# Keeping VectorE's operands in PSUM between the dense stages of a state-space and convolution trunk

## The chip, the core and the metric

The kernel runs on one core of a Trainium2 chip. The metric is the device time of one launch in microseconds (us). TensorE (PE) multiplies matrices and writes its results to PSUM, of which the kernel uses eight banks of 128 partitions by 512 float32 numbers; all else lies in SBUF. VectorE (DVE), ScalarE (ACT) and GpSimd (POOL) work element by element; POOL's operands all lie in SBUF here. SyncE (SP) issues most transfers. Each engine takes its own instructions in order, and engines wait for each other by semaphores.

## The reference

Two layers on a sequence of 512 tokens with 1024 features, batch 1, all in float32:

```python
for i in range(DEPTH):                       # DEPTH = 2
    mods = c_act @ w_ada[i] + b_ada[i]
    sh1, sc1, g1, sh2, sc2, g2 = [m[:, None, :] for m in jnp.split(mods, 6, axis=-1)]
    h = modulate(rms_norm(x, norm1_g[i]), sh1, sc1)
    mix = s5_mixer(h, ...) if i % 2 == 0 else short_conv_mixer(h, ...)
    x = x + g1 * mix
    h = modulate(rms_norm(x, norm2_g[i]), sh2, sc2)
    x = x + g2 * swiglu(h, w_ffn_in[i], w_ffn_out[i])
return rms_norm(x, final_g)
```

`rms_norm` divides each token by the root of the mean of its squares. The state-space mixer ends in a gated product (GLU): `val, gate = jnp.split(y @ w_out, 2, axis=-1)` and `val * jax.nn.sigmoid(gate)`. The feed-forward part has 2816 hidden features.

## The kernel before, in words

The residual `xT` lies in SBUF with features on the partitions: eight blocks k of 128 features by 512 tokens. Every dense product is made of three matmuls on float32r halves (`acc3`, L336): the weights are split into a high part `wh` (copied by ACT, L119) and a low part `wl` (subtracted by DVE, or by POOL where `ws.eng` is `e.G`, L109), the activations likewise into `wide` or `hid` and `hlo`. `group` (L342) runs such products into tiles of PSUM called `o0` to `o3`; each tile is a bank. `SL` cuts the tokens: s = 0 is all 512, s = 1 and s = 2 are the halves of 256.

The first part, the state-space mixer with its scan, follows a list written out by hand (`ORDER`). Everything behind it is put in order by the framework's list scheduler, which goes by dependencies and by its own estimates, and which adds the waits. It treats two accesses to one PSUM bank as dependent whichever columns they touch. Behind the list come, in this order, the GLU projection, feed-forward 0, the convolution mixer, feed-forward 1 and the output.

Between two dense stages stands a normalization. So that TensorE does not stand idle there, `transition` (L456) halves the tokens: the last products of a stage are made for s = 1 and then for s = 2 (`tail`), and while those for s = 2 run, the norm of s = 1 is worked out (`Norm`, L426). `fix` adds a finished tile to `xT` (`resid`, L423, or `glu`, L556) and adds its squares to `acc` (`square`, L415). When all eight blocks are in, `sums` (L432) makes the sum over features by a matmul with ones into a bank called `ssq`, `rsqrt_small` (L262) takes the root in eleven small steps of DVE in the tile `nst`, `spread` puts the result on all partitions by a matmul into the bank `rstd`, and `apply` makes `nt` (DVE), `wide` (ACT) and `hlo` (DVE) for each k, from which the next stage's first products start, again s = 1 first (`first`), then s = 2. While s = 1 of the next stage runs, `hook2` works out the norm of s = 2. During transitions POOL subtracts the low weights.

The transition from the GLU projection into feed-forward 0 differs from the others. Its tail has only half the products per block, so its eight half tiles lie two to a bank (`halves`, L453): `o0` to `o3` for s = 1, `t20` to `t23` for s = 2. Blocks 2, 3, 6 and 7 are finished there. For each of them `glu` adds the partial sums `part` to value `pv` and gate `pg`, takes the sigmoid of the gate (ACT, L563), multiplies (DVE), adds to `xT` (DVE, L565) and squares. A chain of these steps for one block and one token half is called a unit below. The units use `pv` and `pg` of tiles `o0`/`o1`, `o0`/`o1` again (second half of the banks), `o2`/`o3` twice, then `t20`/`t21` twice and `t22`/`t23` twice. Blocks 4, 5, 0 and 1 are finished before, at full width, and there POOL adds three of the squares (`GE`).

Of the kernel before, what the change touches and what calls it, by code (L numbers as in the profile page):

```python
# [12 lines left out]
ALU = mybir.AluOpType  # L13
# [4 lines left out]
D = 1024  # L18
# [240 lines left out]
    return y, ops  # L259


def rsqrt_small(e, n, src, scale):  # L262

    h, y, t = e.nst[:, 0, 0:n], e.nst[:, 1, 0:n], e.nst[:, 2, 0:n]
    e.ts(h, src, scale / 2, EPS / 2, ALU.mult, ALU.add)
    e.ts(y.bitcast(I32), h.bitcast(I32), -0.5, float(0x5F3759DF - 0x80400000), ALU.mult, ALU.add)
    for _ in range(3):
        for c in range(n):
            q = slice(c, c + 1)
            e.stt(t[:, q], y[:, q], y[:, q], h[:, q], ALU.mult, ALU.mult)  # L270
        e.stt(y, t, 1.5, y, ALU.subtract, ALU.mult)
    return y
# [3 lines left out]
def hybrid_trunk(ctx: ExitStack, tc, x, c, norm1_g, norm2_g, w_ada, b_ada,  # L276
# [3 lines left out]
    e = common(tc, ctx)  # L280
# [11 lines left out]
    mods, xT = e.mods, e.xT  # L292
# [38 lines left out]
    SL = (slice(0, T), slice(0, TH), slice(TH, T))  # L331

    def width(s):
        return T if s == 0 else TH
# [7 lines left out]
    def group(units, nk, rhs, s, tiles=None, kouter=False, hook=None, first=True, last=True):  # L342

        if tiles is None:
            tiles = [e.ps(f"o{j}") for j in range(2 * len(units))]
        outs = [t[:, 0:width(s)] for t in tiles]
        ks = [(u, kk) for u in range(len(units[0])) for kk in range(units[0][u][0].shape[1])]
        run = lambda j, i: acc3(outs[j], units[j // 2][ks[i][0]], ks[i][1], (j % 2) * P, rhs(i, s),
                                first and i == 0, last and i == len(ks) - 1)
        if kouter:  # L350
            for i in range(len(ks)):
                for j in range(len(tiles)):
                    run(j, i)
                if hook:
                    hook(i)
        else:
            for j in range(len(tiles)):
                for i in range(len(ks)):
                    run(j, i)
                if hook:  # L360
                    hook(j)
        return tiles

    def getu(npairs, nk, interleaved):

        t = ws.get(npairs * nk)
        if interleaved:
            return [[t[k * npairs + q] for k in range(nk)] for q in range(npairs)]
        return [[t[q * nk + k] for k in range(nk)] for q in range(npairs)]

    if 1:
# [5 lines left out]
        def half(kh, tiles=None, first=True, last=True):  # L377

            return group(getu(2, 1, True), 1, lambda k, s: yrhs(4 * kh + k, s), 0, tiles=tiles, kouter=True,
                         first=first, last=last)  # L380
# [25 lines left out]
        tiles = part[2]  # L406
# [3 lines left out]
        def ft(tag, n=T, dt=F32):  # L410
            return fp.tile([P, n], dt, tag=tag, name=tag)

        accs = fp.tile([P, T], F32, tag="acc", bufs=1, name="acc")

        def square(k, s, init=False, eng=None):  # L415
            if init:
                A.activation(out=accs[:, SL[s]], in_=xT[:, k, SL[s]], func=AF.Square)
            else:
                q = ft("sq")[:, 0:width(s)]
                A.activation(out=q, in_=xT[:, k, SL[s]], func=AF.Square)  # L420
                e.add(accs[:, SL[s]], accs[:, SL[s]], q, eng)

        def resid(ps, g, k, s):  # L423
            e.stt(xT[:, k, SL[s]], ps[:, 0:width(s)], g[:, k:k + 1], xT[:, k, SL[s]], ALU.mult, ALU.add)

        class Norm:  # L426
# [5 lines left out]
            def sums(self):  # L432
                self.ps = e.ps("ssq")
                o = (self.s - 1) * TH
                for b in range(2):
                    e.mm(self.ps[:, b:b + 1], accs[:, o + b * P:o + b * P + P], e.ones1[:, 0:1], True, True)
                self.y = rsqrt_small(e, 2, self.ps[:, 0:2], 1.0 / D)

            def spread(self):
                self.r = e.ps("rstd")  # L440
# [12 lines left out]
        def halves(name):  # L453
            return [t[:, h * TH:h * TH + TH] for t in (e.ps(f"{name}{j}") for j in range(4)) for h in range(2)]

        def transition(tail, fix, gs, sh, first, n=4):  # L456


# [6 lines left out]
            for j in range(n):  # L465
                fix(j, tiles, 1)
            t2 = [e.ps(f"t2{j}") for j in range(4)] if n == 4 else halves("t2")

            def hook(j):
                if j == (0 if n == 4 else 3):  # L470
                    n1.sums()
                    ada.finish()
                if j == (2 if n == 4 else 6):
                    n1.spread()
                    n1.apply([0, 1])
                fix(j, t2, 2)
                if j == n - 1:
                    n1.apply(range(2, 8))
# [16 lines left out]
        class Ffn:  # L495
# [30 lines left out]
            def fix(self, j, tiles, s, k=None):  # L526
                k = 4 + j if k is None else k
                resid(tiles[j], mods[(self.i, 5)], k, s)
                square(k, s, k == 0)

            def tail(self, s, hook, tiles=None):
                if s == 1:
# [23 lines left out]
        def glu(k, pv, pg, s, add=None):  # L556
            g = ft("sg")[:, 0:width(s)]
            pv, pg = pv[:, 0:width(s)], pg[:, 0:width(s)]
            if add:
                e.add(g, pg, add[1])  # L560
                e.add(add[0], pv, add[0])
                pg, pv = g, add[0]
            A.activation(out=g, in_=pg, func=AF.Sigmoid)  # L563
            e.mul(g, g, pv)
            e.stt(xT[:, k, SL[s]], g, mods[(0, 2)][:, k:k + 1], xT[:, k, SL[s]], ALU.mult, ALU.add)  # L565
            square(k, s, k == 4, GE if s == 0 else None)

        GE = e.G
        ws.eng = e.G
        ada.finish()  # L570
        half(1, tiles=tiles, first=False)
        for q in range(2):
            glu(4 + q, tiles[q], tiles[2 + q], 0)
        tiles = half(1)
        for q in range(2):
            glu(q, tiles[q], tiles[2 + q], 0, (part[0][:, q], part[0][:, 2 + q]))
# [8 lines left out]
        def glu_fix(j, tiles, s):  # L585
            q, o = j % 4 - 2, (1, 3)[j // 4]
            if q >= 0:
                glu(2 * o + q, tiles[j - 2], tiles[j], s, (part[o][:, q, SL[s]], part[o][:, 2 + q, SL[s]]))
# [52 lines left out]
        for o in range(PAIRS):  # L641
            if o:
                if o == 2:
                    zbig(1)
                tiles = group(getu(2, 2, True), 2, rhs, 0, kouter=True)
# [7 lines left out]
        def conv_fix(j, tiles, s, k=None):  # L653
            k = 4 + j if k is None else k
            resid(tiles[j], mods[(1, 2)], k, s)
            square(k, s, k == 0)

        for o in range(2):
            tiles = group(getu(1, 2, False), 2, zrhs, 0, kouter=True)
            for j in range(2):  # L660
                conv_fix(j, tiles, 0, 2 * o + j)
            ada.step(16)
# [8 lines left out]

        f1 = Ffn(1)
        hi, lo, rhs = transition(conv_tail, conv_fix, mods[(1, 4)], mods[(1, 3)], f1.first)
        f1.body(rhs, 0)

# [30 lines left out]
        tiles = f1.tail(1, None)  # L706
# [761 lines left out]
```

## Time and profile before

| what | value |
|---|---|
| time, median of 3 runs | 1162.95 us (1160.84 to 1164.36) |
| time of the profiled execution | 1161.99 us |
| its span, first to last instruction | 1160.2 us |
| TensorE busy in the span | 1105.0 us, 95% |
| VectorE busy | 644.9 us, 56% |
| ScalarE busy | 384.6 us, 33% |
| GpSimd busy | 180.6 us, 16% |
| mean granted TensorE clock | 0.986 |

The span is what the profiler sees between the first and the last instruction, and the device time lies 1.8 us around it. The clock is the share of full speed that was granted to TensorE. An idle time in brackets behind a row says how long the engine stood before that instruction and whose end released it. An engine's busy time says little here by itself: what counts is where TensorE stands still or runs at half clock.

### The profile page before, as it was taken

To read this page: it belongs to the slowest core of one execution; us is meant where nothing else is said; L and a number is where in the kernel's file an instruction comes from. 1 tells how busy PE (TensorE), PEld (TensorE's weight loads), DVE (VectorE), ACT (ScalarE), POOL (GpSimd) and SP (SyncE) were. 2 spreads that over 40 slices of the span, in tenths; PEclk is the share of its full clock that TensorE was granted. 3 is DMA by queue.
4 is the path that set the end of the run, shared out by engine and by line. 5 is a ranking of instruction groups with operands and counts; after the bars stand their busy time and mean duration, and the time that the engine had idled before them with its cause. 6 is when DMAs were issued, how large, how long until landed. Compare 5 with 4: busy or idle time off the path is not lost.

```text
span 1160.2 us, 16331 instructions
## 1 busy us (share of the span) xinstructions
PE 1105.0 (95%) x6516; PEld 932.1 (80%) x6516; DVE 644.9 (56%) x1250; ACT 384.6 (33%) x596; POOL 180.6 (16%) x134
## 2 busy tenths in 40 slices
PE   4788999899999999999999999999999999999996
PEld 2566778898888888888889888899888888888886
DVE  8898323975666267733687665757324324233244
ACT  4754344342231132222334242334223213222233
POOL 4797817400000000000050000031000000000000
PEclk9889999999999999999999999999999999999999
DMA  9337654218894398726723939512332332233102
GB/s 279 126 115 255 195 192 127 91 55 182 195 193 120 118 193 197 182 90 137 173 92 105 202 112 210 151 61 86 109 110 88 95 108 88 94 109 100 55 28 73
DMA packets 141851, 153.50 MB, mean 132 GB/s; under 512 B 8288, under 2 KB 129228, under 8 KB 141776
## 3 DMA queue, kind: packets, MB, share of 16 engines
q1 hardware_dynamic: 140672, 150.79, 48.3%
q10 hardware_dynamic: 816, 1.58, 0.5%
q8 instruction: 51, 0.84, 0.3%
q14 instruction: 24, 0.20, 0.1%
q0 software_dynamic: 288, 0.10, 0.1%
HBM read 147.99 MB, written 2.10 MB: 129 GB/s over the span
## 4 chain that ended last, share of the span: by engine, by line
PE 85%; DVE 11%; ACT 3%; issue 1%; DMA 0%; DVEq 0%; ACTq 0%
PE o L117 79%; PE t L117 2%; DVE sx L109 1%; DVE scq L109 1%; DVE sg L109 1%; DVE xT L115 1%; DVE hlo L115 1%; DVE acc L109 1%; PE gmm L117 1%; PE yps L117 1%; DVE sr L120 0%; PE xtp L118 0%; DVE scr L109 0%; DVE v L109 0%; ACT u L1202 0%
## 5 line engine op out<-in xcount | busy, mean ns | idle before, releaser
L117 PE MATMUL o<-wide,wh 128*128 128x512 f32 (+1 forms) x992 | 364.7, 371 | 1.8 <-ACT wide L450 1.8
L117 PE MATMUL o<-wide,wl 128*128 128x512 f32 (+1 forms) x992 | 363.8, 370 | 0.0
L117 PE MATMUL o<-hlo,wh 128*128 128x512 f32 (+1 forms) x992 | 354.9, 370 | 2.3 <-DVE hlo L115 2.2
L119 ACT ACTIVATE wh<-wr 128x1024 fp32r<-128x1024 f32 (+1 forms) x184 | 188.5, 1039 | 387.1 <-PE o L117 310.0
L109 DVE TENSOR_TENSOR wl<-wr,wh 128x1024 fp32r<-128x1024 f32 (+1 forms) x156 | 185.4, 1199 | 157.3 <-ACT wh L119 155.3
L117 PEld LDWEIGHTS o<-wide,wh 128*128 128x128 f32 x992 | 187.9, 189 | 33.2 <-ACT wide L450 2.6
L117 PEld LDWEIGHTS o<-wide,wl 128*128 128x128 f32 x992 | 187.9, 189 | 30.8
L117 PEld LDWEIGHTS o<-hlo,wh 128*128 128x128 f32 x992 | 182.9, 189 | 34.7 <-DVE hlo L115 3.1
L117 PE MATMUL o<-hid,wh 128*128 128x512 f32 (+1 forms) x704 | 205.6, 375 | 0.0
L109 POOL TENSOR_TENSOR wl<-wr,wh 128x1024 fp32r<-128x1024 f32 x28 | 68.5, 2465 | 571.6 <-ACT wh L119 561.8
L117 PEld LDWEIGHTS o<-hid,wh 128*128 128x128 f32 x704 | 129.3, 188 | 23.7
L117 PE MATMUL o<-hid,wl 128*128 128x512 f32 (+1 forms) x352 | 131.9, 375 | 0.0
L109 DVE TENSOR_TENSOR sg<-sg,o 128x512 f32<-128x512 f32 (+1 forms) x50 | 31.8, 644 | 167.0 <-PE o L117 164.2
L115 DVE SCALAR_TENSOR_TENSOR aacc<-ada,cper,aacc 128x256 f32<-128x256 f32 x217 | 108.4, 499 | 21.7 <-DMA ada<-in_w_ada_dram 15.8
L506 ACT ACTIVATE sg<-o 128x512 f32<-128x512 f32 (+1 forms) x48 | 26.8, 562 | 170.3 <-PE o L117 168.6
L117 PEld LDWEIGHTS o<-hid,wl 128*128 128x128 f32 x352 | 66.3, 188 | 11.9
L117 PE MATMUL o<-yT,wh 128*128 128x512 f32 (+1 forms) x256 | 73.0, 367 | 0.0
L115 DVE SCALAR_TENSOR_TENSOR xT<-o,mod,xT 128x512 f32<-128x512 f32 (+1 forms) x56 | 38.7, 693 | 56.6 <-PE o L117 56.4
L117 PEld LDWEIGHTS o<-yT,wh 128*128 128x128 f32 x256 | 46.1, 189 | 8.4 <-issue 0.4
L117 PE MATMUL o<-yT,wl 128*128 128x512 f32 (+1 forms) x128 | 46.5, 363 | 0.0
L420 ACT ACTIVATE sq<-xT 128x256 f32<-128x256 f32 (+1 forms) x44 | 20.6, 472 | 57.3 <-DVE xT L115 51.7
L109 DVE TENSOR_TENSOR acc<-acc,sq 128x256 f32<-128x256 f32 (+1 forms) x41 | 26.5, 647 | 13.3 <-ACT sq L420 13.1
(219 smaller groups left out, 1024.9 us busy)
## 6 DMA issues: line engine op xcount, KB each, us to landing
wr<-in_w_ffn_in_dram SPq DMA_DIRECT2D x88, 512.0 KB, 3.5
ada<-in_w_ada_dram SPq DMA_DIRECT2D x112, 256.0 KB, 9.2
wr<-in_w_ffn_out_dram SPq DMA_DIRECT2D x40, 512.0 KB, 3.7
gt<-in_w_ada_dram SPq DMA_DIRECT2D x12, 1024.0 KB, 5.4
wr<-in_conv_w_in_dram SPq DMA_DIRECT2D x24, 512.0 KB, 3.5
aw<-in_w_ada_dram SPq DMA_DIRECT2D x16, 512.0 KB, 8.8
wr<-in_ssm_w_out_dram SPq DMA_DIRECT2D x16, 512.0 KB, 6.4
wr<-in_conv_w_out_dram SPq DMA_DIRECT2D x8, 512.0 KB, 6.3
```

What stands on the lines that cost most here:

```text
L109: (eng or e.V).tensor_tensor(out=out, in0=a, in1=b, op=op)
L115: e.stt = lambda o, a, s, b, op0, op1: e.V.scalar_tensor_tensor(out=o, in0=a, scalar=s, in1=b, op0=op0, op1=op1)
L117: e.mm = lambda o, l, r, start, stop: e.PE.matmul(out=o, lhsT=l, rhs=r, start=start, stop=stop)
L119: e.cp = lambda o, i: e.A.activation(out=o, in_=i, func=AF.Copy)
L420: A.activation(out=q, in_=xT[:, k, SL[s]], func=AF.Square)
L506: A.activation(out=w, in_=g[:, 0:width(s)], func=AF.Silu)
```

## The change

Intermediate results of the transitions stay in the PSUM banks of tiles that are finished anyway, so that each of DVE's sums, products and residual steps has one operand in PSUM and one in SBUF, where some had both in SBUF. `rsqrt_small` keeps its scaled sum and its products in the bank `ssq` and only the root in `nst`. `square` lets ACT write the squares over the finished tile, and DVE adds them from there; POOL's three additions are DVE's now. `glu` adds the partial sums in place, in the banks of `pv` and `pg`, multiplies into `pv` and squares into `pg`.

```diff
-def rsqrt_small(e, n, src, scale):
-
-    h, y, t = e.nst[:, 0, 0:n], e.nst[:, 1, 0:n], e.nst[:, 2, 0:n]
+def rsqrt_small(e, n, ps, scale):
+
+
+    src, h, y, t = ps[:, 0:n], ps[:, 8:8 + n], e.nst[:, 1, 0:n], ps[:, 16:16 + n]
     e.ts(h, src, scale / 2, EPS / 2, ALU.mult, ALU.add)
...
-        def square(k, s, init=False, eng=None):
+        def square(k, s, ps, init=False):
+
             if init:
                 A.activation(out=accs[:, SL[s]], in_=xT[:, k, SL[s]], func=AF.Square)
             else:
-                q = ft("sq")[:, 0:width(s)]
+                q = ps[:, 0:width(s)]
                 A.activation(out=q, in_=xT[:, k, SL[s]], func=AF.Square)
-                e.add(accs[:, SL[s]], accs[:, SL[s]], q, eng)
+                e.add(accs[:, SL[s]], accs[:, SL[s]], q)
...
-                square(k, s, k == 0)
+                square(k, s, tiles[j], k == 0)
...
             if add:
-                e.add(g, pg, add[1])
-                e.add(add[0], pv, add[0])
-                pg, pv = g, add[0]
+                e.add(pg, pg, add[1])
+                e.add(pv, pv, add[0])
             A.activation(out=g, in_=pg, func=AF.Sigmoid)
-            e.mul(g, g, pv)
-            e.stt(xT[:, k, SL[s]], g, mods[(0, 2)][:, k:k + 1], xT[:, k, SL[s]], ALU.mult, ALU.add)
-            square(k, s, k == 4, GE if s == 0 else None)
-
-        GE = e.G
+            e.mul(pv, pv, g)
+            e.stt(xT[:, k, SL[s]], pv, mods[(0, 2)][:, k:k + 1], xT[:, k, SL[s]], ALU.mult, ALU.add)
+            square(k, s, pg, k == 4)
+
```

The scheduler puts the instructions in another order for it, on TensorE too. First VectorE in the units on `o2` and `o3`, in the tail for s = 1 of the GLU transition; `part` are the partial sums, `sg` the sigmoid or the product, `sq` the squares. Before:

```order
L109 TENSOR_TENSOR part3_2044<-o2_2290,part3_2044 128x256
L109 TENSOR_TENSOR acc_2083<-acc_2083,sq_2403 128x256
L109 TENSOR_TENSOR sg_2406<-o3_2291,part3_2044 128x256
L109 TENSOR_TENSOR sg_2415<-o3_2291,part3_2044 128x256
L109 TENSOR_TENSOR sg_2406<-sg_2406,part3_2044 128x256
L109 TENSOR_TENSOR sg_2415<-sg_2415,part3_2044 128x256
L115 SCALAR_TENSOR_TENSOR xT_70<-sg_2406,mod02_78,xT_70 128x256
L115 SCALAR_TENSOR_TENSOR xT_70<-sg_2415,mod02_78,xT_70 128x256
```

And in the changed kernel:

```order
L109 TENSOR_TENSOR o3_2288<-o3_2288,part3_2044 128x256
L109 TENSOR_TENSOR acc_2083<-acc_2083,o1_2286 128x256
L109 TENSOR_TENSOR o2_2287<-o2_2287,sg_2401 128x256
L115 SCALAR_TENSOR_TENSOR xT_70<-o2_2287,mod02_78,xT_70 128x256
L109 TENSOR_TENSOR o2_2287<-o2_2287,part3_2044 128x256
L109 TENSOR_TENSOR acc_2083<-acc_2083,o3_2288 128x256
L109 TENSOR_TENSOR t20_2417<-t20_2417,part1_1721 128x256
L109 TENSOR_TENSOR o3_2288<-o3_2288,part3_2044 128x256
L109 TENSOR_TENSOR t21_2418<-t21_2418,part1_1721 128x256
L109 TENSOR_TENSOR o2_2287<-o2_2287,sg_2409 128x256
L115 SCALAR_TENSOR_TENSOR xT_70<-o2_2287,mod02_78,xT_70 128x256
```

Before, the two units on a pair of banks go side by side, step by step. Now the second unit's addition to `o3` stands behind the first unit's last access to `o3`, the sum of squares.

Second, TensorE where the first norm comes back (`rstd`) in the same transition; `o0` to `o3` are then the first tiles of feed-forward 0. Before:

```order
L117 MATMUL t23_2427<-yT11_1982,wh15_2192 128x256
L117 MATMUL rstd_2544<-ident_67,nst_77 128x128 x2
L117 MATMUL t23_2427<-yT10_1981,wh15_2192 128x256
L117 MATMUL t23_2427<-yT10_1981,wl15_2193 128x256
L117 MATMUL t23_2427<-yT11_1982,wh15_2192 128x256
```

And in the changed kernel:

```order
L117 MATMUL t23_2420<-yT11_1982,wh15_2191 128x256
L117 MATMUL rstd_2535<-ident_67,nst_77 128x128 x2
L117 MATMUL o0_2622<-wide_69,wh16_2197 128x256
L117 MATMUL o0_2622<-wide_69,wl16_2198 128x256
L117 MATMUL o1_2623<-wide_69,wh16_2197 128x256
L117 MATMUL o1_2623<-wide_69,wl16_2198 128x256
L117 MATMUL o2_2624<-wide_69,wh17_2273 128x256
L117 MATMUL o2_2624<-wide_69,wl17_2274 128x256
L117 MATMUL o0_2622<-hlo0_2271,wh16_2197 128x256
```

The twelve products for the second half of `t23` have moved 44 rows back, into the first group of the feed-forward.

Third, TensorE and VectorE around the norm of s = 2. Before, TensorE makes its sums here, and the matmuls into `rstd` come 41 rows later, ahead of the products for s = 2:

```order
L117 MATMUL o3_2636<-wide_69,wl19_2610 128x256
L117 MATMUL ssq_2673<-ones1_68,acc_2083 128x1 x2
L117 MATMUL o0_2633<-hlo1_2275,wh18_2282 128x256
L117 MATMUL o1_2634<-hlo1_2275,wh18_2282 128x256
L117 MATMUL o2_2635<-hlo1_2275,wh19_2609 128x256
```

In the changed kernel both stand together behind the last product for s = 1:

```order
L117 MATMUL o3_2625<-wide_69,wl19_2599 128x256
L117 MATMUL o3_2625<-hlo1_2272,wh19_2598 128x256
L117 MATMUL ssq_2662<-ones1_68,acc_2083 128x1 x2
L117 MATMUL rstd_2712<-ident_67,nst_77 128x128 x2
L117 MATMUL o0_2782<-wide_69,wh16_2197 128x256
```

And VectorE there in the changed kernel; before, the steps of the root all stood ahead of the products `sg` of feed-forward 0:

```order
L109 TENSOR_TENSOR acc_2083<-acc_2083,t23_2420 128x256
L109 TENSOR_TENSOR sg_2772<-sg_2772,o2_2624 128x256
L109 TENSOR_TENSOR sg_2777<-sg_2777,o3_2625 128x256
L116 TENSOR_SCALAR ssq_2662<-ssq_2662 128x2
L116 TENSOR_SCALAR nst_77<-ssq_2662 128x2
L109 TENSOR_TENSOR hid0_2771<-sg_2772,hid0_2771 128x256
L115 SCALAR_TENSOR_TENSOR ssq_2662<-nst_77,ssq_2662 128x1
L109 TENSOR_TENSOR hid0_2771<-sg_2777,hid0_2771 128x256
L115 SCALAR_TENSOR_TENSOR ssq_2662<-nst_77,ssq_2662 128x1
L115 SCALAR_TENSOR_TENSOR nst_77<-ssq_2662,nst_77 128x2
```

So nothing of the feed-forward's first group is left behind the sums for TensorE to do, and VectorE takes four steps of that group's evacuation in between.

More of the change, by code (lines that the diff above doesn't have):

```diff
@@ L436, in sums @@
                     e.mm(self.ps[:, b:b + 1], accs[:, o + b * P:o + b * P + P], e.ones1[:, 0:1], True, True)
-                self.y = rsqrt_small(e, 2, self.ps[:, 0:2], 1.0 / D)
+                self.y = rsqrt_small(e, 2, self.ps, 1.0 / D)
             def spread(self):
@@ L655, in conv_fix @@
             resid(tiles[j], mods[(1, 2)], k, s)
-            square(k, s, k == 0)
+            square(k, s, tiles[j], k == 0)
         for o in range(2):
```

## The prediction

> **What bounds the kernel now.** The page says that TensorE is busy for 95% of the span and carries 85% of the chain that ended last.
>
> ```profile
> PE 1105.0 (95%) x6516; PEld 932.1 (80%) x6516; DVE 644.9 (56%) x1250; ACT 384.6 (33%) x596; POOL 180.6 (16%) x134
> PE 85%; DVE 11%; ACT 3%; issue 1%; DMA 0%; DVEq 0%; ACTq 0%
> ```
>
> So a shorter step of DVE is worth nothing by itself; what counts is when the results arrive for which TensorE stands. Next I cut the span at the places where TensorE stands. The first two columns are a stretch and its length, the third TensorE's busy time; the granted clock is the third number from the end.
>
> ```profile
> 62.71:66.12 3.41, 1.57 (x24) 1.12 (x18) 3.34 (x15) 0.59 (x1) 3.33 (x3) 1.00 0.17 44
> 66.12:69.54 3.42, 3.42 (x42) 3.15 (x42) 2.74 (x9) 1.68 (x3) 3.26 (x4) 0.50 0.80 240
> 223.14:226.55 3.41, 0.39 (x4) 0.20 (x2) 3.38 (x2) 0.51 (x1) 3.41 (x2) 1.00 0.26 83
> 226.55:233.38 6.83, 5.87 (x27) 5.87 (x28) 6.26 (x13) 4.04 (x9) 2.06 (x2) 0.50 0.35 112
> 250.00:585.00 335.00, 335.00 (x1542) 280.03 (x1541) 193.20 (x298) 90.62 (x114) 4.95 (x2) 1.00 0.67 159
> 585.00:620.00 35.00, 31.92 (x250) 30.36 (x249) 28.18 (x72) 14.12 (x28) 9.75 (x4) 1.00 0.25 79
> 602.02:605.43 3.41, 2.40 (x18) 1.99 (x18) 3.41 (x7) 1.77 (x4) 0.93 (x1) 1.00 0.66 213
> 605.43:608.84 3.41, 2.46 (x21) 2.26 (x20) 3.03 (x4) 0.85 (x3) 2.38 (x1) 1.00 0.13 43
> 800.00:1110.00 310.00, 310.00 (x1405) 258.31 (x1404) 107.61 (x121) 81.42 (x101) 0.00 (x0) 1.00 0.30 95
> ```
>
> In the dense stages TensorE has no gap, so what it loses in a transition comes off nowhere later. The transition at 585 to 620 loses 3.1 us. The GLU transition, 216 to 246, loses most, and its waits stand in TensorE's own timeline (start, length, in brackets the idle time before and its releaser):
>
> ```profile
> 211.40 0.28 PE L117 MATMUL o<-yT,wh 128*128 128x256 f32 x1
> 215.72 0.28 PE L117 MATMUL t<-yT,wh 128*128 128x256 f32 x1
> 216.65 0.58 PE L117 MATMUL ssq<-ones,acc 128*128 128x1 f32 x4 [0.66 <-DVE acc L109]
> 222.92 0.61 PE L117 MATMUL rstd<-ident,nst 128*128 128x128 f32 x4
> 227.51 0.58 PE L117 MATMUL t<-yT,wh 128*128 128x256 f32 x1 [3.98 <-DVE sg L109]
> 243.32 0.28 PE L117 MATMUL o<-wide,wl 128*128 128x256 f32 x1
> 243.44 0.28 PE L117 MATMUL o<-hlo,wh 128*128 128x256 f32 x1
> 245.31 0.39 PE L117 MATMUL o<-wide,wh 128*128 128x256 f32 x1 [1.15 <-ACT wide L450]
> ```
>
> That is 0.66 + 3.98 + 1.15 = 5.8 us of idling. The 3.98 also cost clock: the 3.41 us in which TensorE worked 0.39 were followed by 6.83 at half clock, with 5.87 us of work in them, of which half, 2.9 us, is lost. In all the stage loses 8.7. The other rows of that table price the clock: 1.57 us of work in a stretch of 3.41 led to half clock too, 2.40 did not. The shortest half-clock stretch costs 3.42/2 = 1.7.
>
> **The change part by part.** *POOL and DVE.* DVE and POOL in the same place:
>
> ```profile
> 215.42 0.42 DVE L109 TENSOR_TENSOR acc<-acc,sq 128x256 f32<-128x256 f32 x1
> 217.34 2.04 DVE L109 TENSOR_TENSOR sg<-sg,part 128x256 f32<-128x256 f32 x1
> 222.16 0.74 DVE L109 TENSOR_TENSOR part<-t,part 128x256 f32<-128x256 f32 x2
> 222.82 1.81 DVE L109 TENSOR_TENSOR sg<-sg,part 128x256 f32<-128x256 f32 x1
> 224.68 2.44 DVE L115 SCALAR_TENSOR_TENSOR xT<-sg,mod,xT 128x256 f32<-128x256 f32 x1
> 227.04 0.41 DVE L109 TENSOR_TENSOR sg<-t,part 128x256 f32<-128x256 f32 x1
> 231.87 2.40 DVE L109 TENSOR_TENSOR acc<-acc,sq 128x256 f32<-128x256 f32 x1 [0.19 <-ACT sq L420]
> 216.71 2.39 POOL L109 TENSOR_TENSOR wl<-wr,wh 128x1024 fp32r<-128x1024 f32 x1 [6.32 <-ACT wh L119]
> 221.98 4.86 POOL L109 TENSOR_TENSOR wl<-wr,wh 128x1024 fp32r<-128x1024 f32 x2 [2.88 <-ACT wh L119]
> 231.61 2.38 POOL L109 TENSOR_TENSOR wl<-wr,wh 128x1024 fp32r<-128x1024 f32 x1 [4.77 <-ACT wh L119]
> ```
>
> A DVE instruction with both operands in SBUF that meets a POOL subtraction ends 0.3 us after POOL does, taking up to 2.4 us for 0.42; one that reads a tile of PSUM (222.16) passes at 0.37 each. The change makes the first kind into the second everywhere but in `hlo`, which still reads `nt` and `wide`. These four stalls, 7.0 us of DVE, go.
>
> *Units.* What one costs now, from the groups nearest to its six steps (partial sum, sigmoid out of PSUM, product, residual, square, sum):
>
> ```profile
> L109 DVE TENSOR_TENSOR part<-o,part 128x256 f32<-128x256 f32 x4 | 1.6, 408 | 0.0
> L506 ACT ACTIVATE sg<-o 128x256 f32<-128x256 f32 x8 | 2.9, 383 | 13.4 <-PE o L117 13.4
> L109 DVE TENSOR_TENSOR sg<-sg,o 128x256 f32<-128x256 f32 x8 | 3.1, 419 | 7.5 <-PE o L117 5.5 <-ACT sg L506 2.1
> L115 DVE SCALAR_TENSOR_TENSOR xT<-o,mod,xT 128x256 f32<-128x256 f32 x12 | 5.8, 480 | 4.5 <-PE o L117 4.5
> L420 ACT ACTIVATE sq<-xT 128x256 f32<-128x256 f32 x32 | 13.2, 415 | 45.4 <-DVE xT L115 39.8 <-DVE nst L116 3.8 <-DVE nst L115 1.8
> ```
>
> 0.41 + 0.38 + 0.42 + 0.48 + 0.42 + 0.42 = 2.53, and with six hand-overs of 0.06 (227.04 + 0.41 to 227.51) 2.9 us. Before, two units on one pair of banks ran side by side; the new order makes the second wait for the last access of the first. TensorE finishes `o3` at 211.40 + 0.28 = 211.7. Two units in series, with t20's sum (0.41) and about 0.7 of other work queued between their steps on DVE and ACT (an estimate: t20's product and residual, 0.90, and a weight copy, less what they overlap), end at 211.7 + 5.8 + 1.1 = 218.6, against 216.65 now. TensorE runs dry at 216.0 as before: **2.6 us idle instead of 0.66.**
>
> [...] Could units go by columns, this term would stay at 0.66.
>
> *First norm.* From the sums to `rstd` TensorE has the same 48 products: 222.92 + 0.61 - 216.65 = 6.9, so it is through at 225.5. The 3.98 is gone, since those products moved back. Next come `nt` and `wide`, the chain that ended in **1.15** idle at 245.31, so 226.65. Then `hlo` is wanted after six products (243.44 - 243.32 = 0.12 each, 0.7). POOL's pair, which starts when TensorE lets go of weight tiles, comes 2.0 later than now, 224.0 to 228.9, and DVE reaches `hlo` at about 227: it passes at 228.9 + 0.3, and **2.0 us idle** follow to 229.3 (0 if it slips in between the pair).
>
> *Second norm.* 96 + 12 - 6 products are left, 12.2 us, to 241.6. In them lie `t23`'s second half, done near 235.5, and its unit: 2.9, behind one more POOL stall of `hlo` (2.0) and some 1.2 of queue, so 241.6 too. Then the sums (0.6), and from there nothing covers:
>
> ```profile
> 220.79 1.13 DVE L115 SCALAR_TENSOR_TENSOR nst<-nst 128x1 f32<-128x1 f32 x6
> 239.06 0.17 DVE L116 TENSOR_SCALAR nst<-nst 128x2 int32<-128x2 int32 x1
> 239.06 1.28 ACT L506 ACT_TABLE_LOAD   x1
> ```
>
> DVE must first make two products of the feed-forward, which wait for ACT: the last square at 241.2, table load 1.28, activation 0.38, products 0.76, so 243.6. The root takes 2 x 0.17 + 3 x 0.57 = 2.1, with two `hid` subtractions between (0.7) to 246.4, `rstd` 0.6, then 1.15: 248.2. TensorE idles 248.2 - 242.2 - 0.6 = **5.4 us instead of 1.15.** I price a step on `ssq` like one on `nst`; a row at +-0.02 each would move 11 steps by 0.2.
>
> [...]
>
> *Sum.* Idle: 2.6 + 1.15 + 2.0 + 5.4 = 11.15, less 5.8: +5.4. Clock: the 2.9 of now goes. The new 6 us with 0.6 of work contain a stretch of 3.41 below 1.57 wherever its edges fall, so that a half-clock stretch follows: +2.9, like now's. The pair 1.15 and 2.0, or the 2.6 before, draws a second in about two of three alignments, 1.7 to 2.9, partly hidden by the waits: +2.1. *Other transitions:* DVE's sums there lose their stalls, but `hlo` keeps its own, and blocks of PSUM are held a little longer: between -3.1 (all idling at 585 to 620 goes) and +1; I take -0.5, as no wait there is released by a sum for long. *Final norm:* its chain swaps sources at equal price, 0. Together 5.4 - 2.9 + 2.9 + 2.1 - 0.5 = **+7.0**, on the profiled execution 1161.99 + 7.0 = 1169.0 (span 1167.2). The median stood 0.96 above that execution, so **1170.0**.
>
> **The rivals.** *Faster, 0.05:* the stalls of DVE were what held TensorE at 227.51; without them the 3.98 and its 2.9 of half clock go and nothing new comes: 1162.95 - 6.9 = 1156. It decides at the sums of the second norm, if they come before TensorE's last product. For that the second unit on `t22` and `t23` would have to be through by 241, which asks for `t23`'s second half on TensorE a good 3 us earlier than the order puts it. [...] Against it speaks the order, in which `rstd` stands right behind `ssq`. *No change, 0.13:* `hlo` slips in between POOL's pair (-2.0), no second half-clock stretch comes (-2.1) and the last is short (-1.2): 1164.7. *Much slower, 0.10:* three steps of a unit read and write one bank, which no row shows. Below nothing has no reason; at most they take double, 1.25 us more per unit; the four units on the path make it +5: 1175. That the change does nothing can't be, since the order shows the new operands on DVE and the moved products on TensorE; what can be is that its moves cancel, and this is the no-change case. *The forecast, 0.72:* 1166.7 (no second half-clock stretch, -2.1, and the last one short, -1.2) to 1174.1 (the other transitions at +1, so +1.5, the second stretch at 2.8, so +0.7, and the queues of 0.7 and 1.2 twice as long, +1.9).
>
> **How the numbers follow.** A measurement can tell 0.3%, 3.5 us, from no change. From the cases: faster 0.05, same 0.13, slower 0.82. The range takes in most of the no-change case and of the in-place cost: 1165 to 1177.
>
> **What would show it.** Right: no DVE stall in sums, products and residuals; idle of 2 to 3 us before `ssq`, rows of 1 and 2 before `wide` and `hlo` products, 4 to 6 around the second `rstd`, and half clock soon after it. Wrong: `ssq` at 216.7, or in-place steps well above 0.42, or a transition at 585 that changes by more than 1 us.

## The result, and the profile after

The changed kernel takes **1171.57 us** in the median of 4 runs (1169.36 to 1175.34), the kernel before beside it 1163.18 (1160.84 to 1164.36). The ratio is 1.0081 with a 95% interval of [1.0058, 1.0104]: 8.4 us slower at the median, where 7 were forecast.

The profiled execution took 1175.34 us, span 1173.4, and is the longest of the four; against it the accounts below come out larger than the medians do. TensorE's waits in the GLU transition (timeline of TensorE, changed kernel; start, length, in brackets the idle time before and its releaser):

```profile
218.54 1.01 PE L117 MATMUL ssq<-ones,acc 128*128 128x1 f32 x4 [2.56 <-DVE acc L109]
229.31 0.39 PE L117 MATMUL o<-wide,wh 128*128 128x256 f32 x1 [1.12 <-ACT wide L452]
232.08 1.01 PE L117 MATMUL o<-hlo,wh 128*128 128x256 f32 x3 [1.79 <-DVE hlo L115]
245.77 0.61 PE L117 MATMUL ssq<-ones,acc 128*128 128x1 f32 x4
250.72 1.20 PE L117 MATMUL rstd<-ident,nst 128*128 128x128 f32 x4 [4.34 <-DVE nst L115]
253.03 0.58 PE L117 MATMUL o<-wide,wh 128*128 128x256 f32 x1 [1.11 <-ACT wide L452]
```

The 3.98 of before is gone, and five others stand there: 2.56 + 1.12 + 1.79 + 4.34 + 1.11 = 10.9 us instead of 5.8. They cost clock as well. The windows view, cut at the edges of the half-clock stretches (length, TensorE's busy time, and third from the end the granted clock):

```profile
214.53:217.94 3.41, 1.45 (x13) 1.24 (x11) 2.62 (x7) 2.10 (x4) 2.17 (x1) 1.00 0.00 0
217.94:224.76 6.82, 6.22 (x29) 6.22 (x30) 3.35 (x15) 0.39 (x1) 0.17 (x1) 0.50 0.24 77
228.18:231.59 3.41, 0.99 (x7) 0.78 (x6) 3.40 (x6) 1.31 (x4) 3.41 (x2) 1.00 0.30 80
231.59:235.00 3.41, 2.92 (x13) 2.92 (x14) 3.41 (x10) 1.62 (x4) 0.15 (x1) 0.50 0.76 228
245.25:248.66 3.41, 1.13 (x10) 0.92 (x8) 2.06 (x8) 2.70 (x6) 0.00 (x0) 1.00 0.25 86
248.66:258.90 10.24, 7.07 (x25) 6.22 (x26) 7.88 (x24) 3.60 (x8) 0.00 (x0) 0.50 0.00 0
```

Three times a stretch of 3.41 us with 1.0 to 1.5 of work is followed by half clock. The work in the slow stretches, 6.22 + 2.92 + 7.07 = 16.2, costs half of itself, 8.1 us, instead of 2.9.

Why the first sums come late is seen on VectorE, in the units on `o2` and `o3` (rows of VectorE's timeline, other work between them left out, and POOL's row of that time, changed kernel):

```profile
211.70 0.43 DVE L109 TENSOR_TENSOR o<-o,part 128x256 f32<-128x256 f32 x1 [0.72 <-PE o L117]
212.58 0.43 DVE L109 TENSOR_TENSOR o<-o,sg 128x256 f32<-128x256 f32 x1
213.05 0.48 DVE L115 SCALAR_TENSOR_TENSOR xT<-o,mod,xT 128x256 f32<-128x256 f32 x1
213.57 0.43 DVE L109 TENSOR_TENSOR o<-o,part 128x256 f32<-128x256 f32 x1
214.05 0.42 DVE L109 TENSOR_TENSOR acc<-acc,o 128x256 f32<-128x256 f32 x1
214.92 0.42 DVE L109 TENSOR_TENSOR o<-o,part 128x256 f32<-128x256 f32 x1
216.36 0.42 DVE L109 TENSOR_TENSOR o<-o,sg 128x256 f32<-128x256 f32 x1
216.81 0.48 DVE L115 SCALAR_TENSOR_TENSOR xT<-o,mod,xT 128x256 f32<-128x256 f32 x1
218.07 0.41 DVE L109 TENSOR_TENSOR acc<-acc,o 128x256 f32<-128x256 f32 x1
215.77 2.35 POOL L109 TENSOR_TENSOR wl<-wr,wh 128x1024 fp32r<-128x1024 f32 x1 [11.03 <-ACT wh L119]
```

Every step takes its 0.41 to 0.48, although POOL subtracts from 215.77 to 218.12. But the first unit runs from 211.70 to 214.47, the end of its sum of squares. The second one's addition to its value had followed the first one's residual step at 213.57, but its addition to the gate, on which the sigmoid waits, comes only behind that sum, at 214.92; the unit ends at 218.48, and the matmul for the sums starts at 218.54.

The rest of the span, here in pieces of equal length around the same waits, the kernel before first and the changed one second:

```profile
585.00:635.00 50.00, 46.92 (x351) 44.33 (x350) 38.82 (x89) 20.90 (x38) 9.75 (x4) 1.00 0.29 91
737.00:752.00 15.00, 15.00 (x70) 12.46 (x69) 12.23 (x18) 6.22 (x8) 0.00 (x0) 1.00 0.61 185
767.00:817.00 50.00, 49.72 (x376) 47.61 (x375) 33.30 (x78) 20.75 (x38) 9.91 (x4) 1.00 0.28 84
```

```profile
585.00:635.00 50.00, 47.03 (x356) 44.72 (x356) 41.36 (x89) 20.69 (x38) 14.59 (x6) 1.00 0.24 75
750.00:765.00 15.00, 13.10 (x59) 10.13 (x58) 12.14 (x18) 6.18 (x8) 0.00 (x0) 1.00 0.62 187
780.00:830.00 50.00, 49.08 (x371) 47.01 (x370) 33.03 (x78) 20.43 (x38) 9.71 (x4) 1.00 0.27 83
```

So against the profiled execution of before: idle in the GLU transition +5.1, half clock there +5.2, the transition at 585 -0.1 (2.97 idle instead of 3.08), the convolution's output +1.9, the last inner transition +0.6 (0.92 instead of 0.28). That is 12.7 of the 13.2 us by which the span is longer. The 1.9 is not the change's, as the experiments show.

### The profile page after: what moved, and what is told of

Read it like the earlier page. It is cut to its first block, busy times and chain, and to the rows that moved or that the text cites. A ratio compares the mean times of both kernels' runs of the same rounds, so it can differ in the third digit from the quotient of the medians.

```text
span 1173.4 us, 16304 instructions
## 1 busy us (share of the span) xinstructions
PE 1112.0 (95%) x6516; PEld 937.4 (80%) x6516; DVE 638.0 (54%) x1253; ACT 384.0 (33%) x596; POOL 175.4 (15%) x131
## 4 chain that ended last, share of the span: by engine, by line
PE 81%; DVE 10%; DMA 4%; ACT 2%; issue 1%; SPq 0%; DVEq 0%; ACTq 0%
PE o L117 74%; PE t L117 3%; DMA ada<-in_w_ada_dram 3%; DVE hlo L115 1%; DVE sx L109 1%; DVE scq L109 1%; PE gmm L117 1%; PE yps L117 1%; DVE aacc L115 1%; DVE wl L109 1%; DVE xT L115 0%; PE xtp L118 0%; DVE nt L115 0%; DVE scr L109 0%; ACT u L1202 0%
## 5 line engine op out<-in xcount | busy, mean ns | idle before, releaser
L115 DVE SCALAR_TENSOR_TENSOR xT<-o,mod,xT 128x512 f32<-128x512 f32 (+1 forms) x64 | 43.5, 683 | 59.2 <-PE o L117 58.7
L115 DVE SCALAR_TENSOR_TENSOR hlo<-nt,mod,wide 128x256 fp32r<-128x256 f32 x48 | 33.8, 732 | 3.5 <-ACT wide L452 3.5
L117 PE MATMUL o<-z,wh 128*128 128x512 f32 (+1 forms) x128 | 32.1, 339 | 1.9 <-ACT z L119 1.6
```

The source lines that it names most:

```text
L115: e.stt = lambda o, a, s, b, op0, op1: e.V.scalar_tensor_tensor(out=o, in0=a, scalar=s, in1=b, op0=op0, op1=op1)
L117: e.mm = lambda o, l, r, start, stop: e.PE.matmul(out=o, lhsT=l, rhs=r, start=start, stop=stop)
```

## The experiments

Theory A is that of the prediction: two units on one pair of banks are put in series, and all that matters happens in the GLU transition. Theory B: steps on PSUM are slow in themselves, in the root and the squares above all. Each kernel was timed in five rounds against the kernel before on the same chip.

**1 and 2: each half of the change alone.** In the first, `glu` is that of before (with `sq` in SBUF and POOL's additions) in the changed kernel; in the second, only `glu` and its squares are changed:

```diff
# 1, from the changed kernel
-                e.add(pg, pg, add[1])
-                e.add(pv, pv, add[0])
+                e.add(g, pg, add[1])
+                e.add(add[0], pv, add[0])
+                pg, pv = g, add[0]
...
-            square(k, s, pg, k == 4)
+            square(k, s, None, k == 4, GE if s == 0 else None)
# 2, from the kernel before
-            square(k, s, k == 4, GE if s == 0 else None)
+            square(k, s, k == 4, ps=pg)
```

> Only the GLU part is undone: partial sums, product and squares of glu go to SBUF again (POOL's three additions too), while the root steps and the squares of the other transitions stay in PSUM. Theory A (two units on one pair of banks are put in series, all of the loss is in the GLU transition): within 2 us of the kernel before, 1161 to 1165, with the waits of before at 216.65 (0.7), 227.5 (4.0) and 245.3 (1.2). Theory B (steps on PSUM, in the root or in the squares, are themselves the cost): at least half of the 8.4 us stays, 1167 or more. Theory C (nothing is lost in the other transitions, they gain what their stalls were worth): 1160 or less.

> The other half: only glu and its squares use PSUM, root steps and the other squares are those of before. Theory A: the whole loss, 1168 to 1174, with waits near 2.6 before the first sums and 4 to 5 before the second norm's spread. Theory B: half of the loss or less, 1167 or less.

Measured: 1163.3 us without the GLU part, ratio 1.0009 [0.9997, 1.0021]; 1172.15 with it alone, 1.008 [1.0052, 1.0108]. The loss is in `glu` and nowhere else. B falls for the root and the other squares, which cost 1.0 us by the ratio (-0.3 to +2.4); the third experiment excludes it for `glu`. TensorE's waits without the GLU part are those of before:

```profile
215.82 0.58 PE L117 MATMUL ssq<-ones,acc 128*128 128x1 f32 x4 [0.66 <-DVE acc L109]
226.69 0.38 PE L117 MATMUL t<-yT,wh 128*128 128x256 f32 x1 [3.98 <-DVE sg L109]
243.61 0.39 PE L117 MATMUL o<-wide,wh 128*128 128x256 f32 x1 [1.11 <-ACT wide L452]
```

The same trace has a wait of 1.27 and one of 0.34 in the convolution's output, like the changed kernel's 1.9. So has the fourth kernel, which has nothing of the change (1.6 and 0.3), while the changed kernel itself has only 0.5 there in its second profile, and five of the other experiments' traces have none. That wait comes and goes with the execution; its cause stays open.

**3 and 4: a bank for each unit.** One line decides which half tiles share a bank. Now value and gate of one unit do, instead of the values of two units and the gates of two units; 3 is the changed kernel with it, 4 the kernel before:

```diff
-            return [t[:, h * TH:h * TH + TH] for t in (e.ps(f"{name}{j}") for j in range(4)) for h in range(2)]
+            t = [e.ps(f"{name}{j}") for j in range(4)]
+            return [t[j // 4 * 2 + j % 2][:, j % 4 // 2 * TH:j % 4 // 2 * TH + TH] for j in range(8)]
```

> The changed kernel with one line more: value and gate of a unit lie in the two halves of one bank, so that no two units share a bank. Theory A: units run side by side again, the 2.6 us before the first sums go to nearly 0 (211.7 + 2.9 + 1.1 is before TensorE runs dry at 216.0), the second half of the last tile has nothing to wait for and comes ahead of the norm, so the 4.3 go to about 1 and most of the half clock goes; idle in the stage 3 to 5 us instead of 10.9: 1154 to 1161, faster than the kernel before. Theory B (the steps on PSUM are slow in themselves, or DVE's extra additions): within 3 us of the changed kernel, 1168 or more.

> The kernel before with the same line alone. Theory A says the sharing costs before too, the 4.0 us at 227.5, in which the second half of a tile waits for the reading of its first; but DVE's stalls behind POOL (2.0 to 2.4 each) remain and then stand in the way, so that a wait of several us comes before the first norm's products: between 1159 and 1166. Theory D (the own bank is all that matters, PSUM operands are worth nothing): as fast as the changed kernel with own banks, within 2 us.

Measured: 1158.23 us for the changed kernel with it, 0.996 [0.9946, 0.9974], 3.9 us faster than the kernel before and 13 faster than the change as it was; 1163.41 for the kernel before with it, 1.002 [1.0005, 1.0035]. Theory A held in both, and D falls: with banks apart, PSUM operands are worth 5.2 us. TensorE's waits with both:

```profile
224.99 0.39 PE L117 MATMUL o<-wide,wh 128*128 128x256 f32 x1 [1.52 <-ACT wide L452]
226.81 0.74 PE L117 MATMUL o<-hlo,wh 128*128 128x256 f32 x4 [0.61 <-DVE hlo L115]
239.64 0.39 PE L117 MATMUL o<-wide,wh 128*128 128x256 f32 x1 [0.99 <-ACT wide L452]
```

3.1 us of idling, with the clock at full speed throughout in this execution. (The twelfth kernel has the same three waits, and its profile has one half-clock stretch here, of 3.41 us.) With the bank line alone TensorE stands 4.05 before the first `rstd`, at 228.58, and 3.33 more before the first `wide` product. In that kernel's VectorE rows a root step that takes 2.22 us for its 0.16 ends just ahead of that `rstd`, and a product that takes 2.13 for 0.42 lies between `rstd` and `nt`:

```profile
226.30 2.22 DVE L115 SCALAR_TENSOR_TENSOR nst<-nst 128x2 f32<-128x2 f32 x1
228.96 2.13 DVE L109 TENSOR_TENSOR sg<-sg,part 128x256 f32<-128x256 f32 x1
```

**5 and 6: which access holds the bank.** Both start from the changed kernel; 5 takes the squares of `glu` back to SBUF, 6 the partial sums:

```diff
# 5
-            square(k, s, pg, k == 4)
+            square(k, s, None, k == 4)
# 6
-                e.add(pg, pg, add[1])
-                e.add(pv, pv, add[0])
-            A.activation(out=g, in_=pg, func=AF.Sigmoid)
-            e.mul(pv, pv, g)
+                e.add(add[1], pg, add[1])
+                e.add(add[0], pv, add[0])
+            A.activation(out=g, in_=add[1] if add else pg, func=AF.Sigmoid)
+            e.mul(pv, add[0] if add else pv, g)
```

> The changed kernel, but the squares of glu go to a tile in SBUF again; sums and products of glu stay in place in PSUM. Theory A1 (what puts the units in series is above all the square, which keeps the gate's bank until the very end of a unit): the next unit can begin on the gate's bank after the sigmoid and on the value's after the residual step, some 1.0 us earlier per unit; the wait of 2.6 shrinks to 1 to 1.6 and the second norm's comes down too, as its sums come before TensorE's last product; 1157 to 1166. Theory A2 (steps in place on a shared bank are enough): most of the loss stays, 1168 to 1174.

> The changed kernel, but the partial sums go to SBUF as before (read once from PSUM), while the product is still written into the value's bank and the square into the gate's. Theory A1: the square still holds the gate's bank, and the next unit's sum, which reads it, waits as long: 1167 to 1175. Rival (writing in place, the sums above all, is what costs): 1160 to 1165.

Measured: 1162.11 us with the squares in SBUF, 0.9999 [0.9988, 1.0011]; 1173.03 with the partial sums there, 1.0094 [1.0076, 1.0112]. So it is the square, written over the gate at the end of a unit, that does the damage; summing in place does none that shows. The wait before the first sums is 4.70 us in the sixth kernel, longer than the 2.56 of the change, but hardly by the square alone: its products have both operands in SBUF again, and in the kernel before one such product took 2.04 us beside POOL (217.34). The fifth is the cleaner of the two. In the fifth, the second half of the last tile is back ahead of the norm, and nothing above 2.4 is left:

```profile
216.17 0.39 PE L117 MATMUL t<-yT,wh 128*128 128x256 f32 x1 [1.09 <-ACT sg L564]
223.99 0.71 PE L117 MATMUL rstd<-ident,nst 128*128 128x128 f32 x4 [1.36 <-DVE nst L115]
231.22 0.75 PE L117 MATMUL o<-hlo,wh 128*128 128x256 f32 x4 [1.25 <-DVE hlo L115]
242.41 0.39 PE L117 MATMUL o<-wide,wh 128*128 128x256 f32 x1 [2.37 <-ACT wide L452]
```

**7 and 8: POOL out of the GLU transition.** The low weights of this one transition, six, of which four fall into the stretch in question, are subtracted by VectorE; 7 from the kernel before, 8 from the third kernel:

```diff
-            keep, ws.eng = ws.eng, e.G
+            keep, ws.eng = ws.eng, e.G if n == 4 else None
```

> The kernel before, with the four low weights of the GLU transition subtracted by DVE (1.2 us each) instead of POOL. If DVE's stalls are made by POOL: the additions and products with both operands in SBUF take 0.42 everywhere in the stage, 7 us less for 4.8 us more work, and the wait of 4.0 at 227.5, which ended with such a product, gets shorter: 1156 to 1162. If the stalls have another cause they stay, and the extra work comes on top: 1163 to 1168.

> The changed kernel with a bank per unit (1158.2 measured) and the four low weights on DVE as well. Only the hlo steps can gain there, 0.8 us (1.73 for two where 0.87 is usual), against 4.8 us more work on DVE ahead of the norm: same or slower, 1158 to 1163. If POOL still costs DVE more than these rows show: below 1157.

Measured: 1158.21 us from the kernel before, 0.996 [0.9943, 0.9977]; 1164.19 from the own-bank kernel, 1.0011 [0.9996, 1.0026], 1.2 above the upper end expected at 1163. In the seventh the products with both operands in SBUF take 0.42 and the subtraction costs VectorE 1.22:

```profile
216.68 1.22 DVE L109 TENSOR_TENSOR wl<-wr,wh 128x1024 fp32r<-128x1024 f32 x1
217.88 0.42 DVE L109 TENSOR_TENSOR sg<-sg,part 128x256 f32<-128x256 f32 x1
```

So the stalls are POOL's, and there are two ways to be rid of them for the same 3.9 us: operands in PSUM with a bank for each unit, or no POOL. Together they lose: little is left to gain, and three of the subtractions lie between the first norm's root steps, so that TensorE stands 4.27 us before `rstd`. (That profile is of the fastest of its twelve executions, 1160.67 us.)

**9 and 10: the share of the clock.** 9 is the changed kernel again; 10 has products without a reader in the wait of the second norm:

```diff
+                if warm:
+                    r = e.ps("rstd")
+                    for _ in range(warm):
+                        e.mm(r[:, 0:P], accs[:, o:o + P], e.ident, True, True)
                 self.y = rsqrt_small(e, 2, self.ps, 1.0 / D)
...
-                    n2.sums()
+                    n2.sums(13 if n == 8 else 0)
```

> The changed kernel once more, unchanged, for a narrower interval and a second profile: 1169.5 to 1173.5. The idle times of TensorE should come back to within 0.1 us; what differs from execution to execution should be the half clock, whose stretches begin elsewhere.

> The changed kernel with 13 extra products on TensorE, whose result nobody reads, into the bank rstd between the second norm's sums and its spread (about 0.3 us each by the 0.60 of two spreads, 3.9 in the wait of 4.3). The idle time is thus filled but not shortened. If the half clock behind that wait comes from TensorE standing still, the stretch with 7.1 us of work at half speed goes or shrinks: 1.5 to 3.5 us less than the changed kernel beside it, 1167.5 to 1170. If it comes from anything else: no less, or 0.5 more.

Measured: 1172.77 us, 1.0085 [1.0063, 1.0107], and 1169.76, 1.0066 [1.0049, 1.0083]: 3.0 less at the median, though the two intervals overlap. The idle times of 9 came back to within 0.01 us of the first profile's (2.56, 1.12, 1.80, 4.34 and 1.11). The windows around that wait, the plain kernel first (its stretches start elsewhere than in the first profile), then the one kept busy:

```profile
248.58:251.99 3.41, 0.00 (x0) 0.00 (x0) 3.13 (x15) 0.91 (x3) 0.00 (x0) 1.00 0.00 0
251.99:258.81 6.82, 5.47 (x18) 4.73 (x19) 4.89 (x13) 2.72 (x6) 0.00 (x0) 0.50 0.00 0
```

```profile
247.47:250.88 3.41, 1.45 (x11) 1.06 (x9) 2.36 (x11) 0.17 (x1) 0.00 (x0) 1.00 0.00 0
250.88:254.30 3.42, 3.02 (x11) 2.83 (x12) 3.05 (x8) 1.65 (x4) 0.00 (x0) 0.50 0.00 0
```

The 13 products took 3.15 us, less than the 3.9 estimated, so 1.25 of waiting stayed, then 1.11 more, and one half-clock stretch still came; but it holds 3.02 us of work instead of 5.47 (7.07 in the first profile), 1.2 to 2.0 us saved in these executions. So with the wait filled the slow time behind it is shorter, as expected; the gain in time is not settled by these runs. That the half clock goes with the length of TensorE's waits rests on the work per stretch in several traces (last section).

**11 and 12: own bank without root, and with it.** 11 has the new `glu` and the bank line but root and other squares of before; 12 adds the root steps in PSUM:

```diff
-    h, y, t = e.nst[:, 0, 0:n], e.nst[:, 1, 0:n], e.nst[:, 2, 0:n]
+    src, h, y, t = ps[:, 0:n], ps[:, 8:8 + n], e.nst[:, 1, 0:n], ps[:, 16:16 + n]
```

> GLU part with PSUM operands and a bank per unit, root steps and the other squares as before. If root and other squares are worth nothing, as the run with the GLU part undone says: within 1.5 us of the own-bank run of the whole change, 1156.7 to 1159.7. If nine root steps on PSUM cost 0.4 us on each chain that stands alone: 0.5 to 1.5 less than that, 1156.5 to 1157.7.

> The kernel of the run before (GLU part in PSUM, a bank per unit, 1161.9) with the root's steps in the bank ssq as well; only the squares of the other transitions are still in SBUF. In that run two stretches of root steps, all in SBUF, stalled behind POOL (one step of 0.16 took 2.15 us, seven of 1.3 took 3.23) and TensorE stood 2.0 and 2.1 us behind them. If that is what separates it from the own-bank run of the whole change (1158.2): 1157 to 1159.5, with no such stall and idle times of about 1.5, 0.6 and 1.0 in the stage. If it is the squares of the other transitions: 1161 to 1163.

Measured: 1161.91 us, 1.0004 [0.9993, 1.0015], 2.2 beyond what either view had expected; then 1158.45, 0.9966 [0.995, 0.9983]. The expectation for 11 fell: I had taken the first experiment, in which root and squares were worth nothing, to hold with banks apart too. VectorE's rows of the eleventh kernel, then POOL's, then VectorE's of the twelfth show why it doesn't:

```profile
218.64 2.15 DVE L116 TENSOR_SCALAR nst<-nst 128x2 int32<-128x2 int32 x1
222.03 3.23 DVE L115 SCALAR_TENSOR_TENSOR nst<-nst 128x2 f32<-128x2 f32 x7
```

```profile
218.37 2.40 POOL L109 TENSOR_TENSOR wl<-wr,wh 128x1024 fp32r<-128x1024 f32 x1 [0.47 <-ACT wh L119]
221.69 2.38 POOL L109 TENSOR_TENSOR wl<-wr,wh 128x1024 fp32r<-128x1024 f32 x1 [0.92 <-ACT wh L119]
```

```profile
218.59 0.15 DVE L116 TENSOR_SCALAR nst<-ssq 128x2 int32<-128x2 int32 x1
```

A root step with two numbers per partition stands behind POOL as long as a whole product does: 2.15 us here and 2.22 in the fourth kernel, where a product took 2.13. With units side by side the root's steps meet two of POOL's subtractions, so they need an operand in PSUM too. In the kernel before, and likewise in the first experiment, nearly all of them fall between two subtractions (steps from 219.31 to 221.92, POOL at work until 219.10 and again from 221.98), and there was nothing to save. Other squares add nothing (1158.45 with them in SBUF, 1158.23 without).

No version went below these; the third is the best that was run, 1158.23 us, beside the seventh, 1158.21, which needs no PSUM at all.

## Why the prediction was right

- **Units in series.** 2.6 us were forecast before the first sums, 2.56 came, and the third experiment takes them away with the shared bank alone. The prediction named the last access, the sum of squares, as what the second unit waits for; the fifth and sixth show that it is the decisive one.
- **First norm.** Forecast 1.15 and 2.0; measured 1.12 and 1.79. `hlo` did pass right behind POOL's pair. All of it came 2.7 to 2.8 us later than worked out, as the clock was at half speed from 217.94 on.
- **Second norm.** Forecast 5.4 from the end of the sums to `wide`, less the 0.6 of `rstd`; measured 4.34 + 1.11 = 5.45. Idle together: 11.15 forecast, 10.9 measured.
- **Clock: the term that was mis-sized.** The forecast had the old stretch replaced by one of 2.9 and a second worth 2.1. So +2.1 was forecast, and +5.2 measured in the first profile, +4.6 in the second: three stretches came in both, worth 8.1 us in the first and 7.5 in the second (half of 3.41, 6.19 and 5.47 of work). The second, "in about two of three alignments", was reckoned for the pair or the 2.6 as alternatives: each drew its own, in the second and the tenth kernel too. The last, taken to be like before's 6.83, was so in the second profile; in the first it lasted 10.24.
- **The sum, and luck.** The +7.0 was worked out for the profiled execution, and there the change cost 13.4 us (1175.34 - 1161.99). That 8.4 at the median lies so near the forecast is in part luck: the other three executions took 1169.36 to 1172.19 at a granted clock of 0.983 to 0.985, against 0.980, so they had less half clock, and the 1.9 of the convolution's output, which nobody forecast, comes and goes.
- **DVE.** Sums, products and residuals no longer stall; `hlo` does (one in 2.33 us, two in 2.73), as forecast. The gain of some 7 us on VectorE did not show in the time: TensorE waited for other things. With own banks PSUM operands were worth 5.2 us of time.
- **Price of the steps.** In place on PSUM costs nothing to speak of: 430 and 429 ns for the additions where 408 to 420 were taken; the rival that doubled them falls. The root on `ssq` was taken at 0.2 more at most; where it stands alone, as in the final norm, which was put at 0, it costs 0.4 (below).
- **Other transitions.** Forecast -0.5; the first experiment gives +1.0 (-0.3 to +2.4). At 585 nothing moved by more than 0.1. The +0.6 near 797 is the root's: the twelfth kernel, with old squares, has the wait of 0.76 there as well.

The rival that ended faster was right on what held TensorE at 227.51: with POOL out of the kernel before, the seventh experiment, the 3.98 there is 0.77, the stage has no half clock in the profile, and 3.9 us are gained. It was wrong that nothing new comes: the units in series took more than the stalls gave back. While POOL subtracts, sums, products and residuals with one operand in PSUM take 0.41 to 0.48 here (changed kernel, 215.77 to 218.12); the root's integer step, whose only operand lies in SBUF, took 2.15 us (eleventh experiment).

## What to carry to other kernels

Before an intermediate result is left in a PSUM bank, ask who else lives in that bank and how long the last access to it is away: a result parked there lengthens the bank's occupation to the end of the chain, and puts the neighbour's chain behind it. Give each chain a bank of its own and the same change turns from a loss of 0.8% into a gain of 0.4%. The waits were put in by a scheduler that takes a bank for one thing; whether two engines could use different columns of a bank at once, no run here tried. And price an idle time of TensorE with the half clock behind it: in the profiled execution 5.1 us more idling came with 5.2 us more lost to half clock.

## What the hardware showed beside this

VectorE's groups in place on PSUM, from the changed kernel, and its root steps where nothing lies between them, before and after (final norm):

```profile
L109 DVE TENSOR_TENSOR t<-t,part 128x256 f32<-128x256 f32 x8 | 3.4, 430 | 6.9 <-PE t L117 6.7
L109 DVE TENSOR_TENSOR o<-o,part 128x256 f32<-128x256 f32 x8 | 3.3, 429 | 1.5 <-PE o L117 1.4
```

```profile
1150.51 1.71 DVE L115 SCALAR_TENSOR_TENSOR nst<-nst 128x1 f32<-128x1 f32 x9
```

```profile
1163.66 0.48 DVE L115 SCALAR_TENSOR_TENSOR ssq<-nst,ssq 128x1 f32<-128x1 f32 x2
1164.37 0.48 DVE L115 SCALAR_TENSOR_TENSOR ssq<-nst,ssq 128x1 f32<-128x1 f32 x2
```

A round of the root begins 0.71 us after the last (1164.37 - 1163.66) where it took 1.71 / 3 = 0.57: 0.4 us for three rounds, the price of tiny steps that hand over through PSUM. A single step is hardly longer (221 ns where it was 216); the time lies between the steps.

That an integer step with a single operand in SBUF, two numbers wide, takes 2.15 us beside POOL was not expected. In the eleventh kernel it began at 218.64, 0.27 us into a subtraction of 2.40, and ended at 220.79, 0.02 behind it; in the kernel before, with POOL at rest (219.31), the same step took 0.15.

The half clock needs no standstill: stretches with 0.99, 1.13 and 1.45 us of work in 3.41 were followed by it. The half-clock stretches of one execution begin whole multiples of 3.41 apart: in the changed kernel 217.94, 231.59 and 248.66 are 4 and 5 steps apart (13.65 and 17.07), and one at 1163.43 fits the same grid. Cut on that grid, from where the record of the clock begins (21.75 and 23.38), the profile of the kernel before and the first one of the changed kernel show two edges. At full clock, every stretch of 3.41 us with 1.57 us of TensorE's work or less was followed by half clock, and none with 1.97 or more; between these both occur (1.92 in the kernel before at 21.75 was not, 1.96 in the changed kernel at 1160.02 was, and so was 1.79 in the twelfth at 224.39). At half clock it takes more work to come back: in the changed kernel 2.81 us (217.94) was not enough, 2.92 (231.59) was. The grid of one execution lies elsewhere in the next: the last stretch began 2.06 us before `rstd` in the first profile, at 248.66, and 0.2 before it in the second, at 251.99.
